# A hybrid decoder layer on one core: product order and gates of the feed-forward, buffers of its down stage, key norms and block inverses of RWKV

## Chip, cores and metric

The kernel runs on 1 core of one Trainium2 chip. The metric is the device time of one execution in microseconds; before the change it is 2186.93 us, the median of 3 runs (2183.86 to 2192.37).

## What is computed

One decoder layer on 1024 tokens of width 1024 in float32: a SwiGLU feed-forward, a mixer, a second feed-forward, each added to the residual, and a final norm. The mixer splits into eight heads of RWKV-7 (a delta-rule recurrence) and a spatial gating unit in chunks of 128 tokens. Cut to what the change touches:

```python
x = x + 0.5 * swiglu(rmsnorm(x, g), w1, w3, w2)     # (silu(h@w1) * (h@w3)) @ w2, twice in the layer
kk = heads(k * k_k)
kk = kk / jnp.maximum(jnp.sqrt(jnp.sum(kk * kk, axis=-1, keepdims=True)), 1e-12)
# per head and token: S_t = S_{t-1} diag(decay_t) + (S_{t-1} a_t) b_t^T + v_t k_t^T ;  y_t = S_t r_t
y = rwkv7_scan(rh, heads(decay), kh, vh, -kk, kk * ah)
```

## The kernel before, in words

Every dense product runs in a split form: an operand is stored as a rounded high part and a low rest (a ScalarE cast and a subtraction on VectorE or GpSimd, the "split"), and three matmuls of 128x128 by 512 columns stand for one.

**Feed-forward.** Tokens come in two halves ("rows") of 512, and the products use a Winograd-Strassen form with seven products. Product 1 and 2 of the way up are made in `first_half` (rows of 512 tokens, eight blocks of weights in turn for w1 and w3, s = 0 to 21), its first part stored to DRAM as `sd`. Meanwhile `build` and `x_build` make the sums of normalised inputs (`xc`) for the other products. Then `up` goes through the 22 weight tiles s (even: w1, odd: w3): `up_prep` takes the weights' sums on VectorE and splits them into five `wup` tiles, TensorE makes products 6, 5, 7, 4, 3 of 12 matmuls each (2.7 us), VectorE adds them to the stored part, and `gate` makes silu of the even tile times the odd one. `out` stores the sums of gated tiles (`hd`). `down` runs seven products of 11 tiles with 12 matmuls each; a tile's weights and inputs land in a `raw` buffer (two of them in the kernel before), are split into `wsp` (four), and after a product VectorE adds the PSUM banks to the residual (line 527). Lines 479 and 480 are the loads, 490 to 493 the splits.

**Mixer.** `w_in_lora`, `w_in_rkv` and `gmlp` make the dense input projection; `pair` (two heads, half the tokens) makes decays, normalised keys and the scaled tensors A, R, B, K. An `Oct` is 128 tokens of all heads: `prep` makes the score matrices and turns, `invert` inverts the 8x8 diagonal blocks on VectorE (by way of DRAM), `merge` joins them to 16, 32 and 64 with small matmuls, `chain` carries the state over chunks of 64, `finish` applies the group norm. `w_out` is the output projection.

**What sets the order.** The program is one generator with side tasks. `Flow` interleaves them by estimated times (the numbers behind `yield`) into one order of matmuls, which TensorE keeps. A planner orders the other engines' instructions; `evac` gives those that read PSUM a higher priority. Each engine works its queue in order. Nearly all loads and stores are issued from SP; RWKV's block moves from ScalarE's queue.

In the second feed-forward `first_half` runs interleaved with the second half of RWKV; at s = 12 at the latest, `second` waits for RWKV, makes the second `w_out` and starts the second `build`.

## Time and profile before

| what | us |
|---|---|
| median of 3 runs | 2186.93 |
| fastest, slowest run | 2183.86, 2192.37 |
| profiled execution | 2188.83 |
| its span, first to last instruction | 2187.0 |
| TensorE busy | 1999.5 (91%) |
| VectorE busy | 1272.0 (58%) |
| GpSimd busy | 987.7 (45%) |
| ScalarE busy | 702.2 (32%) |
| mean granted TensorE clock | 0.956 of full speed |

In the rows, PE is TensorE, PEld its weight loads, DVE VectorE, ACT ScalarE, POOL GpSimd and SP the engine that only issues DMAs; SPq is its queue. L192 is line 192 of the kernel, here the helper that emits every dense matmul, L201 that of the small ones. An operand is written as output<-inputs by the names of the tiles: psd, pse and psc are PSUM banks. A duration of a row with several instructions runs from the first one's start to the last one's end. Matmuls are pipelined, so the busy time of PE is not its peak; some matmul records can be missing.

### The profile page before, as it was taken

The page shows a single profiled execution, that of the slowest core. Times are in us where ns is not written, and L with a number is a line of the kernel's source. Part 1 is how long each engine was busy: PE and PEld are TensorE (multiplying, and loading weights), DVE is VectorE, ACT ScalarE, POOL GpSimd, SP SyncE. Part 2 cuts the span into 40 slices and gives each one's busy share as a digit, 9 for nine tenths or more (in the row PEclk, how much of TensorE's full clock was granted, in tenths as well). Part 3 has the DMA queues.
Part 4 walks back from the last instruction along what each step waited for, and adds up shares of the span by engine and source line. Part 5 has one row for each costly group of instructions (what it writes and reads, how often), then busy time and mean ns, then how long its engine had stood idle before and what let it go on. Part 6 is the DMA issues. An engine that isn't in the chain of part 4 may idle for free.

```text
span 2187.0 us, 34516 instructions
## 1 busy us (share of the span) xinstructions
PE 1999.5 (91%) x13408; PEld 1617.7 (74%) x13408; DVE 1272.0 (58%) x1749; ACT 702.2 (32%) x1202; POOL 987.7 (45%) x749
## 2 busy tenths in 40 slices
PE   6999999997998998999999989989789999979986
PEld 5777777786776677777888778867577777858764
DVE  7828777745457464454543354324877777544565
ACT  5442222213444443252212232224422222224432
POOL 4426666643444664353322232223566666434432
PEclk9999999998998999998999997999989999989988
DMA  6754444435544577453534463336644444375443
GB/s 217 239 170 160 151 160 164 165 141 209 187 135 150 180 258 218 114 202 106 172 101 118 121 191 109 119 112 211 223 148 148 148 158 164 110 251 181 133 153 116
DMA packets 232884, 356.15 MB, mean 163 GB/s; under 512 B 67984, under 2 KB 100752, under 8 KB 232720
## 3 DMA queue, kind: packets, MB, share of 16 engines
q1 hardware_dynamic: 178944, 338.23, 46.5%
q10 hardware_dynamic: 53776, 15.71, 3.1%
q8 instruction: 105, 1.72, 0.3%
q14 instruction: 59, 0.48, 0.1%
HBM read 260.53 MB, written 93.34 MB: 162 GB/s over the span
## 4 chain that ended last, share of the span: by engine, by line
PE 22%; DMA 11%; DVE 8%; issue 5%; POOL 3%; ACT 1%; SPq 0%; POOLq 0%; ACTq 0%; DVEq 0%
PE psd L192 12%; PE pse L192 4%; PE pse L201 3%; DMA raw<-in_ffn_w_dram 3%; DMA raw<-hd 2%; PE psc L201 2%; DMA wraw<-in_ffn_w_dram 1%; POOL wsp L493 1%; DMA raw<-in_w_out_dram 1%; POOL wsp L712 1%; DVE wsp L492 1%; DVE rd L527 1%; POOL wup L257 1%; DMA tdr<-D 1%; DMA M<-ldr 1%
## 5 line engine op out<-in xcount | busy, mean ns | idle before, releaser
L192 PE MATMUL psd<-xt,wsp 128*128 128x512 f32 x1920 | 484.7, 408 | 19.4 <-ACT silu L353 9.0
L192 PEld LDWEIGHTS psd<-xt,wsp 128*128 128x128 f32 x1920 | 363.6, 193 | 115.7 <-ACT silu L353 12.1
L192 PE MATMUL psd<-xc,wup 128*128 128x512 f32 x1584 | 376.0, 394 | 37.2 <-DVE z L447 20.3
L192 PEld LDWEIGHTS psd<-xc,wup 128*128 128x128 f32 x1584 | 298.0, 189 | 108.7 <-DVE z L447 23.8
L712 POOL TENSOR_TENSOR wsp<-raw,wsp 128x512 fp32r<-128x512 f32 x170 | 234.3, 1398 | 317.7 <-ACT wsp L709 317.5
L192 PE MATMUL psd<-wsp 128*128 128x512 f32 x1440 | 351.0, 402 | 27.4 <-ACT wsp L491 14.9
L192 PEld LDWEIGHTS psd<-wsp 128*128 128x128 f32 x1440 | 274.0, 193 | 97.5 <-ACT wsp L491 16.7
L493 POOL TENSOR_TENSOR wsp<-raw,wsp 128x512 fp32r<-128x512 f32 x154 | 210.3, 1368 | 293.7 <-ACT wsp L491 241.3
L257 POOL TENSOR_TENSOR wup<-wraw,wup 128x512 fp32r<-128x512 f32 x132 | 200.6, 1528 | 117.7 <-ACT wup L256 112.4
L192 PE MATMUL pse<-xc,wup 128*128 128x512 f32 x1056 | 248.0, 390 | 0.0
L192 PEld LDWEIGHTS pse<-xc,wup 128*128 128x128 f32 x1056 | 198.4, 188 | 41.4 <-ACT wup L256 0.2
L709 ACT CAST wsp<-raw 128x512 fp32r<-128x512 f32 x246 | 140.5, 618 | 152.5 <-PE psd L192 58.2
L492 DVE TENSOR_TENSOR wsp<-raw,wsp 128x512 fp32r<-128x512 f32 x110 | 96.2, 876 | 104.8 <-ACT wsp L490 104.3
L256 ACT CAST wup<-wraw 128x512 fp32r<-128x512 f32 x132 | 81.1, 619 | 223.5 <-PE pse L192 151.8
L192 PE MATMUL pse<-wsp 128*128 128x512 f32 x396 | 118.3, 416 | 31.2 <-DVE wsp L492 18.1
L491 ACT CAST wsp<-raw 128x512 fp32r<-128x512 f32 x154 | 95.4, 620 | 124.2 <-DMA raw<-hd 114.2
L490 ACT CAST wsp<-raw 128x512 fp32r<-128x512 f32 x110 | 68.0, 618 | 195.2 <-DMA raw<-in_ffn_w_dram 107.8
L192 PEld LDWEIGHTS pse<-wsp 128*128 128x128 f32 x396 | 75.2, 197 | 59.3 <-DVE wsp L492 22.0
L192 PE MATMUL psc<-wsp 128*128 128x512 f32 x396 | 111.6, 408 | 0.0
L257 POOL TENSOR_TENSOR wup<-wt,wup 128x512 fp32r<-128x512 f32 x44 | 63.4, 1440 | 69.7 <-ACT wup L256 58.7
L256 ACT CAST wup<-wt 128x512 fp32r<-128x512 f32 x88 | 53.6, 617 | 120.3 <-PE psd L192 100.9
L192 PEld LDWEIGHTS psc<-wsp 128*128 128x128 f32 x396 | 78.4, 199 | 17.5
(216 smaller groups left out, 2620.6 us busy)
## 6 DMA issues: line engine op xcount, KB each, us to landing
wraw<-in_ffn_w_dram SPq DMA_DIRECT2D x88, 512.0 KB, 4.5
raw<-hd SPq DMA_DIRECT2D x154, 256.0 KB, 3.3
raw<-in_ffn_w_dram SPq DMA_DIRECT2D x132, 256.0 KB, 3.1
raw<-in_ffn_w_dram SPq DMA_DIRECT2D x44, 512.0 KB, 4.0
raw<-in_w_in_dram SPq DMA_DIRECT2D x36, 512.0 KB, 3.6
hd<-u SPq DMA_DIRECT2D x66, 256.0 KB, 2.0
hd<-s SPq DMA_DIRECT2D x66, 256.0 KB, 2.1
sd<-silu SPq DMA_DIRECT2D x44, 256.0 KB, 3.2
```

What stands on the lines that cost most here:

```text
L192: i = self.nc.tensor.matmul(*args, **kw)
L201: i = self.nc.tensor.matmul(*args, **kw)
L256: nc.scalar.copy(t[:, 0], src)
L257: eng.tensor_tensor(t[:, 1], src, t[:, 0].bitcast(F32), op=ALU.subtract)
L490: nc.scalar.copy(t[:, 0, 0], w)
L491: nc.scalar.copy(t[:, 0, 1], h)
L492: ve.tensor_tensor(t[:, 1, 0], w, t[:, 0, 0].bitcast(F32), op=ALU.subtract)
L493: ge.tensor_tensor(t[:, 1, 1], h, t[:, 0, 1].bitcast(F32), op=ALU.subtract)
L527: ve.scalar_tensor_tensor(rv, sets[y][f], 0.25, rv, op0=ALU.mult, op1=ALU.add)
L709: self.nc.scalar.copy(dst[:, 0, sl], src[:, sl])
L712: eng.tensor_tensor(dst[:, 1, sl], src[:, sl], dst[:, 0, sl].bitcast(F32), op=ALU.subtract)
```

## The change

Feed-forward: `gate` applies silu in one ScalarE instruction (the factor at the end becomes 0.5). `up` takes products in the order 6, 5, 7, 3, and 4 after the next tile's 6, each of 6, 5 and 3 in a bank of its own. `down`, `wtile` and `w_out` have four `raw` buffers; scratch tiles of `squares` move to other pools. The normalised inputs of row 0 are stored once (`xn`) by `apply` and loaded by `x_build` instead of normalising again. The second `build` opens its weight pool first and issues the first weight load before `x_build`.

RWKV: squared norms of the keys come from 16 small matmuls by token; their inverse is applied to the score matrix in the mask product and to `Bt` in its PSUM copy, instead of spreading it back and multiplying it into `a`. The block inverse works on 16x16 blocks in 64 partitions: two 8x8 blocks in one instruction, then their off-diagonal part with two products of 512 elements; `merge` has two levels left.

The diff, cut to its core:

```diff
-CON = [("ident", 128), ("me", 128), ("m8", 32), ("m16", 32), ("m32", 32), ...
+CON = [("ident", 128), ("me", 128), ("m16", 32), ("m32", 32), ...
+RAWB = 4
...
     def gate(self, us, pool, s, key, c):
...
-                nc.scalar.activation(u, c, AF.Tanh, scale=0.5)
-                nc.vector.scalar_tensor_tensor(u, u, 1.0, c, op0=ALU.add, op1=ALU.mult)
+                nc.scalar.activation(u, c, AF.Silu)
...
+        ws[3] = sp(b22, ge)
         ws[4] = sp(b21, ge)
-        ws[3] = sp(b22, ge)
...
-        def z(name="z", bufs=6):
+        def z(name="z", bufs=3):
...
-                s1s[s] = z()
+                s1s[s] = z("s1", 3)
...
+        def tail(s, b, w12):
+            yield from prod(s, 4, b, False, True)
             with self.evac():
-                w12 = z()
-                ve.tensor_add(w12, b, s1)
-            yield from prod(s, 5, c, True, False)
-            yield from prod(s, 7, b, False, True)
-            with self.evac():
-                ve.tensor_add(s1, b, s1)
-                w22 = z()
-                ve.tensor_add(w22, c, s1)
-            self.gate(us, u, s, 22, w22)
-            d = self.psum("d")
-            yield from prod(s, 4, d, True, True)
-            with self.evac():
-                ve.tensor_add(s1, d, s1)
-            self.gate(us, u, s, 21, s1)
-            yield from prod(s, 3, c, False, True)
-            with self.evac():
-                ve.tensor_add(w12, c, w12)
-            self.gate(us, u, s, 12, w12)
+                ve.tensor_add(w12, b, w12)
+            self.gate(us, u, s, 21, w12)
             if s % 2:
                 out(s // 2)
             ws.pop(s)
...
+            a = self.psum("d")
+            yield from prod(s, 6, a, True, True)
+            with self.evac():
+                w12 = s1
+                ve.tensor_add(w12, a, s1)
+            if last is not None:
+                yield from tail(*last)
+            c = self.psum("e")
+            yield from prod(s, 5, c, True, True)
+            with self.evac():
+                v = z()
+                ve.tensor_add(v, c, w12)
+            b = self.psum("d")
+            yield from prod(s, 7, b, True, False)
+            with self.evac():
+                w22 = z()
+                ve.tensor_add(w22, b, v)
+            self.gate(us, u, s, 22, w22)
+            d = self.psum("e")
+            yield from prod(s, 3, d, True, True)
+            with self.evac():
+                ve.tensor_add(v, d, v)
+            self.gate(us, u, s, 12, v)
+            last = (s, b, w12)
+        yield from tail(*last)
...
-            raw = self.ws.tile([P, 2, HALF], F32, name="raw", bufs=2)
+            raw = self.ws.tile([P, 2, HALF], F32, name="raw", bufs=RAWB)
...
-                self.squares(self.xq, accs[row], res[row][kp])
+                self.squares(*((self.ws, accs[1], res[1][kp], "raw", RAWB) if row else (pool, accs[0], res[0][kp])))
...
+            if out is not None:
+                nc.sync.dma_start(out[k], t)
...
-            nc.sync.dma_start(t, src[row][k // 2][:, k % 2])
+            nc.sync.dma_start(t, src[row][k // 2][:, k % 2] if row else self.xn[k])
...
-            for k, t in zip(ks, ts):
-                normed(*k, t)
+            for k, t in zip(ks[:2], ts):
+                ve.scalar_tensor_tensor(t, t, self.v(gain, k[1]), rb[0], op0=ALU.mult, op1=ALU.mult)
...
+        if early:
+            self.pw, self.cpw = self.open("pw")
         pool, cb = self.open("pb")
         yield from stats(pool)
+        if early:
+            self.raw0 = self.up_load(self.pw, w, 0)
         yield from self.x_build(pool, self.xc, src, gain, rb)
...
-                    t = self.xq.tile([P, 2, HALF], F32, name="xs", bufs=2)
-                    ts = [t[:, 0], t[:, 1], self.xtp.tile([P, HALF], F32, name="silu", bufs=3)]
+                    ts = [self.xtp.tile([P, HALF], F32, name="silu", bufs=3) for _ in range(3)]
...
-        ss = self.spread2(sq)
-        i8 = self.sm.tile([P, 8], F32, name="i8")
-        ve.tensor_scalar_max(i8, ss, 1e-24)
+        ss = self.psum("e")
+        for i in range(HALF // CH):
+            for s in HS:
+                self.rmm(ss[s, i:i + 1], lhsT=sq[s, i * CH:(i + 1) * CH], rhs=self.one[s], start=(i == 0), stop=True,
+                         skip_group_check=True)
+        i8 = self.inv[half][:, p]
+        ve.tensor_scalar_max(i8, ss[:, 0:HALF // CH], 1e-24)
...
-        inv = self.back2(i8)
...
-        ve.tensor_mul(a, a, inv)
...
+                    for p in range(PR):
+                        k = self.c0 + i
+                        nc.vector.scalar_tensor_tensor(d[:, p], m[:, p], inv[:, p, k:k + 1], c["me"],
+                                                       op0=ALU.mult, op1=ALU.mult)
...
+            K_.nc.vector.tensor_mul(v(t), v(ps), w)
...
-        M = self.tl("M", 1, (P, 8, 8))
+        M = self.tl("M", 1, (64, 16, 16))
...
-        tmp = self.tl("Dtmp", 1, (P, 49))
+        tmp = self.tl("Y2", 1, (P, NB, CH)).rearrange("p b j -> p (b j)")[0:64]
...
+        for l, r, o in ((D[:, 0, 0:8, 0:8], M[:, 0:8, 8:16], Z), (Z, D[:, 0, 8:16, 8:16], D[:, 0, 0:8, 8:16])):
+            nc.vector.tensor_mul(tv, l.unsqueeze(2).broadcast_to([64, 8, 8, 8]),
+                                 r.rearrange("p j k -> p k j").unsqueeze(1).broadcast_to([64, 8, 8, 8]))
+            nc.vector.tensor_reduce(o, tv, axis=AX.X, op=ALU.add)
+            yield 0.6
...
-        for lvl, bs in enumerate((8, 16, 32)):
+        for lvl, bs in enumerate((16, 32)):
```

## Rows read from the trace of the kernel before

**Rows 1.** stages: start:end, length, busy PE, PEld, DVE, ACT, POOL, clock, DMA share, GB/s

```profile
0.00:160.50 160.50, 138.52 (x576) 110.71 (x576) 99.14 (x118) 73.45 (x126) 61.63 (x48) 0.99 0.61 207
160.50:478.30 317.80, 305.98 (x1335) 249.51 (x1336) 238.68 (x276) 83.58 (x142) 193.36 (x132) 1.00 0.44 150
478.30:738.90 260.60, 231.57 (x938) 180.51 (x937) 145.09 (x191) 97.78 (x163) 113.27 (x89) 0.94 0.55 180
738.90:1460.80 721.90, 678.61 (x7838) 558.89 (x7837) 321.52 (x603) 217.99 (x387) 268.28 (x236) 0.94 0.50 151
1460.80:1593.70 132.90, 105.34 (x439) 82.98 (x437) 83.99 (x98) 55.53 (x96) 63.91 (x44) 0.91 0.62 204
1593.70:1909.80 316.10, 307.15 (x1331) 251.44 (x1332) 233.27 (x275) 80.49 (x135) 185.12 (x126) 0.99 0.41 143
1909.80:2166.00 256.20, 226.69 (x935) 178.38 (x933) 141.19 (x179) 91.28 (x152) 101.10 (x75) 0.95 0.53 174
...
sum 2187.00, PE 1999.55 PEld 1617.71 DVE 1271.96 ACT 702.22 POOL 987.67; mean PE 249.94 PEld 202.21 DVE 158.99 ACT 87.78 POOL 123.46
```

**Rows 2.** chain that ended last, 1570 to 1700 us: start, length, what

```profile
1577.04 8.09 DMA wraw<-in_ffn_w_dram
...
1672.87 8.16 PE psd L192 x36
```

**Rows 3.** who TensorE waited for, whole span: us in total, times, longest

```profile
PE psd L192 <- DVE z L447: 20.3, 12, 2.6
...
PE pse L192 <- DVE wsp L492: 18.1, 5, 4.7
...
PE psd L192 <- ACT wsp L491: 14.9, 3, 7.5
...
PE psd L192 <- ACT wup L256: 9.4, 2, 7.6
...
PE pse L201 <- POOL Y L1243: 7.4, 1, 7.4
...
PE psd L192 <- DVE wup L257: 7.2, 2, 7.0
```

**Rows 4.** timeline of the second up stage: start, length, engine, line, [idle before, releaser]

```profile
1740.14 0.69 DVE L386 TENSOR_TENSOR wt<-wraw 128x512 f32<-128x512 f32 x1 [1.40 <-DMA wraw<-in_ffn_w_dram]
...
1744.14 0.68 DVE L447 TENSOR_TENSOR z<-psd,z 128x512 f32<-128x512 f32 x1
...
1744.88 8.00 PE L192 MATMUL psd<-xc,wup 128*128 128x512 f32 x34 [1.48 <-DVE z L447]
```

**Rows 5.** VectorE's instructions by line: busy, mean ns, idle before

```profile
L328 DVE SCALAR_TENSOR_TENSOR u<-u,z 128x512 f32<-128x512 f32 x66 | 61.6, 937 | 23.9 <-ACT u L327 23.9
L328 DVE SCALAR_TENSOR_TENSOR silu<-silu,psd 128x512 f32<-128x512 f32 x22 | 15.0, 682 | 49.9 <-ACT silu L327 39.4 <-DMA sd<-silu 5.6 <-DMA oC<-xC 4.9
L297 DVE SCALAR_TENSOR_TENSOR nx<-nx,vec,rbk 128x512 f32<-128x512 f32 x32 | 33.1, 1050 | 7.2 <-ACT rbk L280 3.6 <-DMA nx<-xres 3.2 <-DMA nx<-in_x_dram 0.4
```

**Rows 6.** line 1043 on ScalarE: ns min/median/max, first and last start

```profile
L1043 ACT ACT_TABLE_LOAD  x2: 1283/1283/1283, 855.9 to 1139.9; - x2
```

**Rows 7.** who SP's queue waited for, 698 to 738 us

```profile
SPq L479 <- DVE wsp L492: 23.2, 9, 5.9
```

**Rows 8.** the page's DMA issues: count, KB each, median us to landing

```profile
raw<-hd SPq DMA_DIRECT2D x154, 256.0 KB, 3.3
```

**Rows 9.** timeline of the second down stage, after its first product

```profile
1949.93 5.46 DVE L527 SCALAR_TENSOR_TENSOR rd<-psd,rd 128x512 f32<-128x512 f32 x9
...
1956.65 1.22 PE L192 MATMUL pse<-wsp 128*128 128x512 f32 x2 [4.28 <-DVE wsp L492]
```

**Rows 10.** timeline of TensorE: small matmuls of RWKV

```profile
781.21 1.05 PE L201 MATMUL pse<-hm,sq 128*128 128x2 f32 x8
...
786.94 1.09 PE L201 MATMUL pse<-con,i 128*64 128x128 f32 x16
...
1287.69 1.12 PE L201 MATMUL pse<-T,SC 64*64 64x32 f32 x32 [0.70 <-DVE D L1146]
```

More of the change, by code (lines that the diff above doesn't have):

```diff
@@ L221, in rstd, with squares @@
         return r[:, :n]
-    def squares(self, pool, acc, t):
+    def squares(self, pool, acc, t, name="xs", bufs=2):
         nc = self.nc
         with self.evac():
-            s = pool.tile([P, 2, HALF], F32, name="xs", bufs=2)
+            s = pool.tile([P, 2, HALF], F32, name=name, bufs=bufs)
             nc.scalar.activation(s, t, AF.Square, scale=1.0 / 32)
@@ L466, in up @@
             ws.pop(s)
+        u = lambda: z("u", 6)
+        prep(0)
+        last = None
+        for s in range(ns):
+            prep(s + 1)
+            s1 = s1s.pop(s)
+            a = self.psum("d")
[23 more added lines that the diff above has]
+        yield from tail(*last)
     def down(self, pool, w2, res, done):
@@ L526, in down, with build @@
                         rv = res[row][k // 2][:, k % 2]
-                        ve.scalar_tensor_tensor(rv, sets[y][f], 0.25, rv, op0=ALU.mult, op1=ALU.add)
+                        ve.scalar_tensor_tensor(rv, sets[y][f], 0.5, rv, op0=ALU.mult, op1=ALU.add)
                     done(p, row, k)
-    def build(self, src, gain, w, rb, stats, ready):
+    def build(self, src, gain, w, rb, stats, ready, early=False):
         self.px, self.cpx = self.open("px")
@@ L571, in program @@
         self.hd = {p: [self.dr.tile([P, HALF], F32, name=f"hd{p}_{j}") for j in range(NP)] for p in range(1, 8)}
+        self.xn = [self.dr.tile([P, HALF], F32, name=f"xn{k}") for k in range(KT)]
         self.sd = [self.dr.tile([P, HALF], F32, name=f"sd{j}") for j in range(2 * NP)]
@@ L580, in program @@
         x12 = self.halves()
-        rbs = [self.keep(rb)]
-        self.apply(x12, rx, "g1", rb)
+        rbs = []
+        self.apply(x12, rx, "g1", rb, self.xn)
         cb.close()
@@ L661, in second @@
             cm.close()
-            yield from self.w_out(1, xres, accs[1])
+            p1, c1 = self.open("p1")
+            yield from self.w_out(1, xres, accs[1], (p1,))
             def stats2(pool):
-                cxq.close()
-                rb = yield from self.spread(accs[1], "e")
-                rbs2.append(self.keep(rb, pool))
-            flow.spawn(self.build(xres[1], "g2", w2, rbs2, stats2, ("xb", 1)))
+                yield 0.1
+                rbs2.append(self.keep(rb1, pool))
+            rb1 = yield from self.spread(accs[1], "e")
+            c1.close()
+            cxq.close()
+            flow.spawn(self.build(xres[1], "g2", w2, rbs2, stats2, ("xb", 1), True))
         yield from self.first_half(x12, w2, hook)
@@ L714, in wtile @@
     def wtile(self, shape, src, eng=None):
-        raw = self.ws.tile([P] + list(shape), F32, name="raw", bufs=2)
+        raw = self.ws.tile([P] + list(shape), F32, name="raw", bufs=RAWB)
         self.nc.sync.dma_start(raw, src)
@@ L733, in dense_T, with w_out @@
         return o
-    def w_out(self, half, xres, acc):
+    def w_out(self, half, xres, acc, sums):
         nc = self.nc
@@ L745, in w_out @@
             for n, k in enumerate([4, 5, 6, 7, 0, 1, 2, 3]):
-                raw = self.ws.tile([P, 2, HALF], F32, name="raw", bufs=2)
+                raw = self.ws.tile([P, 2, HALF], F32, name="raw", bufs=RAWB)
                 nc.sync.dma_start(raw[:, 0], wv[k, :, hc])
@@ L760, in w_out @@
                         nc.vector.tensor_add(r[:, i], r[:, i], ps[2 * j + i])
-                self.squares(self.xq, acc, r)
+                self.squares(*sums[:1], acc, r, *sums[1:])
                 nc.sync.dma_start(xres[1][half][hf * 2 + j], r)
@@ L786, in mixer_consts @@
         self.omk = lambda i: vc[:, 26 + i:27 + i]
-        self.hm = mp.tile([P, 2], F32, name="hm")
-        nc.scalar.copy(self.hm, self.c["bo"][:, 0::64])
-        self.X = [mp.tile([P, NB, CH], F32, name=f"X{i}") for i in range(3)]
+        self.X = [mp.tile([P, NB, CH], F32, name=f"X{i}") for i in range(2)]
         for x in self.X:
@@ L807, in mixer_consts @@
         nc.gpsimd.memset(self.S, 0.0)
+        self.inv = [mp.tile([P, PR, HALF // CH], F32, name=f"inv{h}") for h in range(2)]
         self.pcc = [mp.tile([P, PR, HALF // CH], F32, name=f"pcc{h}") for h in range(2)]
@@ L899, in wrap @@
             yield y
-    def spread2(self, src):
-        ps = self.psum("e")
-        for t in range(4):
-            self.rmm(ps[:, 2 * t:2 * t + 2], lhsT=src[:, t * P:(t + 1) * P], rhs=self.hm,
-                     start=(t == 0), stop=True, skip_group_check=True)
-        return ps[:, 0:8]
-    def back2(self, small):
-        ps = self.psum("e")
-        for t in range(4):
-            for h in range(2):
-                self.rmm(ps[HS[h], t * P:(t + 1) * P],
-                         lhsT=small[:, 2 * t + h:2 * t + h + 1].broadcast_to([P, CH]), rhs=self.c["ident"],
-                         start=True, stop=True)
-        return ps
     def pair(self, half, p, k, v, r):
@@ L1091, in prep @@
         yield 2.5
+        inv = K_.inv[self.half]
         SC = self.SC = self.tl("SC", 2, (P, 2, NC, PR, 2, CH))
@@ L1113, in prep, with turned @@
         yield 0.5
-    def turned(self, name, X):
+    def turned(self, name, X, scale=None):
         K_ = self.K
@@ L1177, in merge @@
             pt = K_.psum("e", (P, 2, NB, CH // 2))
-            for n in range(1 if lvl == 2 else 2):
+            for n in range(1 if lvl == 1 else 2):
                 for b in range(NB):
@@ L1184, in merge @@
                             K_.rmm(pt[s, 1, b], lhsT=T[s, 0, b], rhs=one(X[s, b], 0), start=True, stop=True)
-            for n in range(1 if lvl == 2 else 2):
+            for n in range(1 if lvl == 1 else 2):
                 d = part(T[:, n], 1 - n)
```

64 lines of the change are left out of this document (34 added, 30 removed).

## The prediction, made before the change was timed

> **What bounds the kernel now.** I read the stages first [rows 1]. TensorE is busy 1999.6 of 2187.0 us, so the only large gains are its idle time, its slow clock and work taken off it. One full-speed matmul of 512 columns costs 8.16 us / 36 = 0.2267 us [rows 2]; its count times that is the floor of a stage:
> - first "up" stage (160.5 to 478.3): 1335 records, floor 302.6, measured 317.8, 15 over;
> - second "up" stage (1593.7 to 1909.8): 1331 records, floor 301.7, measured 316.1, 14 over;
> - "down" stages: 7 products x 11 tiles x 12 = 924 matmuls, floor 209.5; measured 260.6 and 256.2, so 51 and 47 over. The granted clock there is 0.94 and 0.95: (1 - 0.94) x 260.6 = 16 us and 13 us of that can be the slow clock;
> - the mixer (738.9 to 1460.8): 7838 matmuls, mostly small ones of RWKV, between the dense ones;
> - the passage to the second "up" (1460.8 to 1593.7): about 413 big matmuls, 94 us, and 2 us of small ones in 132.9: 37 over.
>
> Then who TensorE waits for [rows 3]. 20.3 us go to the VectorE add of line 447, 18.1 and 14.9 us to the splits of the down stage, 7.5 us of it in one stretch; 9.4 and 7.2 us to the first operands of an up stage. The clock falls after such stretches, so a wait removed returns more than its own length.
>
> **Up: product order.** Product 7 accumulates in the bank that product 6 has filled and line 447 has to read first; between them lies only product 5 (12 x 0.2267 = 2.7 us). VectorE works in order, and in front of line 447 stand the weight sums of the next tile, which wait for their load [rows 4]: line 386 starts at 1740.14 when the load lands, line 447 only at 1744.14, TensorE goes on at 1744.88 after 1.48 us of waiting. In the new order 6 has a bank of its own that nobody needs soon; the only bank accumulated into after a read is that of 7, and product 3 and the next tile's product 6 (5.4 us) lie between the read (w22) and product 4. What delayed line 447 here was about 4 us, so most of these waits disappear. The add count stays at five a tile. The smaller pools (z and s1 3, s 4) hold two z and four s tiles per one or two tiles of 13.6 us; I cost them at nothing, since their last readers are done a tile earlier; if not, a wait is that of a store, some 3 us. I leave 5 us over the floor in each stage: **-10** and **-9** (ends -15 and +5: nothing gained, and a late tile every now and then).
>
> **Gates.** Silu in one ScalarE instruction replaces tanh plus a VectorE instruction: 66 x 0.94 + 22 x 0.68 = 77 us of VectorE work leave [rows 5], all beside TensorE; this only shortens the queue in front of the adds. It is in the numbers of the stages. New table loads: one costs 1283 ns [rows 6]; with two more (silu, and back to tanh for the mixer) +2.6, I write **+2** (0 to +4). The Trainium skill (ScalarE: Activation LUTs, "Table sets") puts exp and tanh into one set, does not name silu there, and says to batch calls by set, which speaks against this edit. By its 2.66 us a switch the same two would be an estimated 5.3 us; no run here shows the drain it counts with the load.
>
> **Down: four raw buffers for two.** A raw buffer is reloaded only after its last split. In product 4 of the first down stage the load's issue waits 23.2 us of 40 for VectorE's split to free a buffer [rows 7]; a load lands 3.3 us after its issue [rows 8], and a pair of buffers must turn round in 2 x 2.72 us. So the stage runs at the rate of the buffers, not of an engine: VectorE, ScalarE and GpSimd are busy 145, 98 and 113 of 260.6 us [rows 1]. With four, loads run two tiles further ahead. At the start, loads of the residual and of the eleven dt tiles stand in front, and TensorE waits up to 7.5 us [rows 3]; two tiles more in hand cover 5.4 us of it. Between products nine to twelve evacuations occupy VectorE (nine took 5.46 us, then TensorE had waited 4.28 us for a split [rows 9]); more splits can stand ready (four, 10.9 us). What I leave: 2 us at the start, 4 at the evacuations, 5 for the statistics matmuls, 5 ragged, 7 of clock: 23 of 51. **-28**, and **-26** for the second. In product 4 of the first stage one raw buffer holds the sums of squares of row 1, leaving three. Ends: -10 (the start cover alone) and -36 for each.
>
> **Mixer.** Merge level 8 goes: 96 matmuls an octet, 8 octets. 32 of them take 1.12 us [rows 10], so 96 x 8 / 32 x 1.12 = 27 us of TensorE. The Trainium skill (TensorE: Matmul & The Clock Gate, Part 1) states a floor of about 25 ns from start to start; by it the same 768 would be an estimated 19 us, while the row here gives 35 ns each. The key norms lose 8 matmuls (1.05 us) and 16 (1.09 us) a pair and get 32 small ones (nearest row 1.12 us): -2.14 + 1.12, times 8 pairs, -8 us. Together 35 us off TensorE's stream, which is busy 678.6 of 721.9 us here. VectorE gets the 8 x 8 products of the inverse (two of 512 elements and their sums, about 0.7 us each by the 512-element row of 0.68 us [rows 5]), the Bt scaling and masks in quarters, loses 3 merge evacuations and one product by the norm; it is busy 45%, so only latency counts: about +3 us of VectorE and -4.5 us of a merge level for each octet, equal within 2 us. Bt leaves ScalarE's queue, where it stood behind DMA issues: a small gain. Against: lora_up's three silu tiles serve one iteration instead of two, 8 iterations behind a store of some 3.3 us [rows 8], 26 us of ScalarE waiting at most, mostly under prepared splits: +4; and the scratch of the inverse shares the buffer Y2 with the group norm: 0 to 5 us for each of 8 octets, I take +1 in all. Sum **-30** (ends -50 and +5, this also being a stage whose hand-written order shifts).
>
> **Passage to the second up.** The build of its inputs runs on VectorE; 16 of 32 normalising products (33.1 us / 32 = 1.03 us each [rows 5]) leave, eight of them here: -8 us. The weights' load is issued only after the build and takes 8.09 us [rows 2]; TensorE waits for the operands 7.6 and 7.0 us [rows 3]. It now starts before the build: -12. Four raw buffers in the output projection: -2. **-22** (-30 to -6).
>
> **Start** (0 to 160.5): eight normalising products and eleven gate instructions less on VectorE (16 us) beside TensorE; **-4** (-10 to +4). The 16 stores of 256 KB of normalised inputs run on SP's queue at DMA shares of 0.61 and 0.62 [rows 1]: nothing; if they get in front of weight loads, one landing, 3 us. End (from 2166.0): 0.
>
> **Sum.** -4 -10 -28 -30 -22 -9 -26 +2 = -127. The profiled execution took 2188.8 us (span 2187.0), so 2062; it lies 1.9 above the median of 2186.93: **2060**.
>
> **Rivals.**
> 1. *The downs stay as they are.* Splits and evacuations in one VectorE queue, not the buffers, set the pace; only the start's cover of 5 us each remains. 54 - 10 = 44 back: **2104**. For it: the waits for VectorE's split of 4.28 us after evacuations. Against: that engine is busy little over half of the stage, and the issue waits for a buffer.
> 2. *The mixer gives nothing.* TensorE's stream is shorter, but waits for the same chain (oct load, inverse, merge, chain, norm) and for Y2; in the row with 7.4 us it waits for GpSimd's norm product at the very end [rows 3]. **2090**.
> 3. *Slower.* In the new order the read of w22 falls behind the weight sums on VectorE, in every tile. Whatever it is late beyond the 5.4 us of cover, TensorE stands, 44 times; 127 / 44 = 2.9 us, so from a read 8.3 us late in every tile the whole gain is gone; at 10 us it is 44 x 4.6 = 202 us in place of the 19 hoped for: about **2280**. Against: the delay seen is 4 us, with fewer VectorE instructions to come.
> 4. *It is not what the stages wait for:* every wait is replaced and the time stays at **2187**.
>
> **How the numbers follow.** Forecast 0.66 (own range 2022 to 2095), rival 1 0.15, rival 2 0.13, rival 3 0.04, rival 4 0.02. The range takes in the forecast, rival 2 and most of rival 1: 2020 to 2112. About 0.5% (11 us) is what a measurement of this kernel can tell from no change; so faster 0.94, same 0.02, slower 0.04.
>
> **What would show it.** Right: no waits on the first add of a tile, up stages at 307 us; down stages near 232 with a clock of 0.97 or more; 768 matmuls fewer of the 64x32 form; the weights' load of the second up before its build. Wrong: SP's loads no longer waiting for buffers but down stages still at 250 (rival 1), the mixer at 720 with longer waits (rival 2), waits for w22's add of several us in each tile (rival 3).

## The result, and the profile after

The kernel after takes 2123.4 us (median; 2119.3 to 2130.3), the kernel before, timed beside it, 2185.4 (2178.1 to 2192.4): ratio 0.972, 95% interval 0.968 to 0.976. It is 62 us faster, where 127 were forecast (2060), and lies above the range of 2020 to 2112. The profiled execution took 2130.3 us, span 2128.5; it is the longest of the four runs, 7 us above their median. Every row of a stage below is of one execution, up to 7.5 us from the median of its kernel. The kernel before had medians from 2180.8 to 2185.4 us beside the different runs, so two totals that lie less than 5 us apart are not told apart.

The stages of the kernel after, with columns as in [rows 1] (start:end, length, busy time of TensorE, its loads, VectorE, ScalarE and GpSimd, granted clock, DMA share, GB/s):

```profile
0.00:158.50 158.50, 136.51 (x576) 112.31 (x576) 85.57 (x99) 73.64 (x126) 59.02 (x48) 0.99 0.68 229
158.50:461.10 302.60, 302.35 (x1332) 249.94 (x1333) 187.29 (x243) 84.25 (x142) 175.84 (x129) 1.00 0.48 159
461.10:702.90 241.80, 220.54 (x939) 178.74 (x940) 158.42 (x190) 93.91 (x161) 127.54 (x91) 0.95 0.57 192
702.90:1451.30 748.40, 659.99 (x7137) 545.69 (x7137) 354.24 (x652) 216.41 (x382) 276.36 (x236) 0.90 0.51 149
1451.30:1574.50 123.20, 106.88 (x434) 86.55 (x432) 74.27 (x85) 51.53 (x90) 54.34 (x38) 0.90 0.61 205
1574.50:1878.70 304.20, 303.29 (x1332) 249.69 (x1333) 185.32 (x243) 82.93 (x142) 178.43 (x129) 1.00 0.48 158
1878.70:2108.60 229.90, 219.82 (x937) 178.96 (x936) 146.48 (x179) 89.49 (x153) 114.89 (x78) 0.96 0.56 188
```

Line by line against [rows 1], measured and forecast:

```
stage        before   after   change   forecast
start         160.5   158.5     -2.0      -4
first up      317.8   302.6    -15.2     -10
first down    260.6   241.8    -18.8     -28
mixer         721.9   748.4    +26.5     -30
passage       132.9   123.2     -9.7     -22
second up     316.1   304.2    -11.9      -9
second down   256.2   229.9    -26.3     -26
```

Outside the mixer the stages give -84 where -99 was forecast (+2 more were allowed for table loads). The mixer alone is 56 us off. In its row TensorE has 701 instructions and 18.6 us of busy time less than before, and yet the stage is longer: idle time rose from 43 to 88 us, and the granted clock fell from 0.94 to 0.90. The stretches at 1.2 GHz add up to 150 us there, before to 85. The question of the experiments is therefore where the 35 us of TensorE work went.

Whom TensorE waits for in the mixer of the kernel after (waiting instruction, releaser: us in all, times, longest):

```profile
PE pse L202 <- DMA AR<-xR: 9.3, 3, 3.2
PE pse L202 <- POOL Y L1273: 7.6, 2, 7.4
PE pse L202 <- DVE D L1169: 7.4, 2, 6.3
PE pse L202 <- issue: 6.7, 2, 6.2
PE pse L202 <- DVE SC L1107: 6.4, 4, 2.8
```

No one wait took over. The norm product Y cost the kernel before as much (7.4 us [rows 3]), and so did the loads of AR:

```profile
PE pse L201 <- DMA AR<-xR: 9.3, 3, 5.1
```

New or longer are many small ones on VectorE's steps: the inverse (D), the masks (SC), and more of about 5 us and less.

### The profile page after: what moved, and what is told of

It reads as the page before. It is cut to its first block, busy times and chain, and to the rows that moved or that the text cites. A ratio compares the mean times of both kernels' runs of the same rounds, so it can differ in the third digit from the quotient of the medians.

```text
span 2128.5 us, 33099 instructions
## 1 busy us (share of the span) xinstructions
PE 1954.6 (92%) x12704; PEld 1606.7 (75%) x12704; DVE 1200.3 (56%) x1701; ACT 693.7 (33%) x1194; POOL 987.4 (46%) x748
## 5 line engine op out<-in xcount | busy, mean ns | idle before, releaser
L193 PEld LDWEIGHTS psd<-xt,wsp 128*128 128x128 f32 x1920 | 374.9, 198 | 103.7 <-DVE wsp L731 5.5
L731 POOL TENSOR_TENSOR wsp<-raw,wsp 128x512 fp32r<-128x512 f32 x170 | 237.2, 1415 | 326.3 <-ACT wsp L728 326.2
L193 PE MATMUL psd<-wsp 128*128 128x512 f32 x1440 | 344.9, 400 | 15.2 <-ACT wsp L501 9.3
L503 POOL TENSOR_TENSOR wsp<-raw,wsp 128x512 fp32r<-128x512 f32 x154 | 230.2, 1500 | 214.7 <-ACT wsp L501 165.7
L193 PE MATMUL pse<-xc,wup 128*128 128x512 f32 x1056 | 254.4, 389 | 0.0
L258 POOL TENSOR_TENSOR wup<-wraw,wup 128x512 fp32r<-128x512 f32 x132 | 180.5, 1378 | 118.2 <-ACT wup L257 117.3
L502 DVE TENSOR_TENSOR wsp<-raw,wsp 128x512 fp32r<-128x512 f32 x110 | 107.3, 986 | 79.9 <-ACT wsp L500 79.5
L385 DVE TENSOR_TENSOR wt<-wraw 128x512 f32<-128x512 f32 x44 | 42.1, 957 | 187.7 <-DMA wraw<-in_ffn_w_dram 187.7
L500 ACT CAST wsp<-raw 128x512 fp32r<-128x512 f32 x110 | 68.2, 620 | 185.8 <-PE psd L193 57.8
L193 PE MATMUL pse<-wsp 128*128 128x512 f32 x396 | 113.0, 414 | 14.0 <-DVE wsp L502 8.7
L193 PE MATMUL psc<-wsp 128*128 128x512 f32 x396 | 105.8, 396 | 1.8 <-DVE wsp L502 1.8
L731 DVE TENSOR_TENSOR wsp<-raw,wsp 128x512 fp32r<-128x512 f32 x76 | 63.9, 872 | 75.3 <-ACT wsp L728 71.4
L193 PEld LDWEIGHTS pse<-wsp 128*128 128x128 f32 x396 | 78.5, 201 | 34.8 <-DVE wsp L502 12.3
```

What stands on the lines that cost most here:

```text
L193: i = self.nc.tensor.matmul(*args, **kw)
L258: eng.tensor_tensor(t[:, 1], src, t[:, 0].bitcast(F32), op=ALU.subtract)
L385: ve.tensor_sub(t1, b12, b11)
L500: nc.scalar.copy(t[:, 0, 0], w)
L502: ve.tensor_tensor(t[:, 1, 0], w, t[:, 0, 0].bitcast(F32), op=ALU.subtract)
L503: ge.tensor_tensor(t[:, 1, 1], h, t[:, 0, 1].bitcast(F32), op=ALU.subtract)
```

## Experiments 1: the parts one by one

V is the inverse from blocks of 16, N the key norms by token, F all of the feed-forward part (gates, order of products, buffers, row statistics).

**V undone** (e1_no_v): `invert`, `merge` and the constants as before.

```diff
-        for lvl, bs in enumerate((16, 32)):
+        for lvl, bs in enumerate((8, 16, 32)):
...
-        M = self.tl("M", 1, (64, 16, 16))
+        M = self.tl("M", 1, (P, 8, 8))
...
```

> The kernel after, but with inverses from blocks of 8 and three merge levels as before (key norms by token and all of the feed-forward part stay). Theory P (pace: the mixer is as long as its chain of RWKV steps; work taken off TensorE comes back as waits): 2123 +- 8 us, mixer 740 to 755 us, TensorE busy there about 25 us more than the 660 of the kernel after and idle as much less. Theory V (the longer inverse on 64 partitions, 9.2 us in place of 4.4 for each octet, is what the mixer lost): 2095 to 2105, mixer about 720. Theory N (key norms by token cost it): 2123 + 0 to 25. Theory F (the feed-forward part's side effects on the mixer cost some 55 us, and the RWKV part gives the forecast 30): about 2145, mixer 770.

**N undone** (e2_no_n): `pair`, the mask products and `turned` as before.

```diff
-        ss = self.psum("e")
-        for i in range(HALF // CH):
...
+        ss = self.spread2(sq)
...
+        inv = self.back2(i8)
...
```

> The kernel after, but with the key norms as before (eight spreading and sixteen back-spreading products a pair, one mask product for each B half, Bt copied by ScalarE); the inverse from blocks of 16 and the feed-forward part stay. Theory P: 2123 +- 8 us, mixer 740 to 755. Theory N (masks in quarters and Bt on VectorE lengthen the way to the inverse): 2095 to 2110, mixer 720 to 735. Theory V: 2123 to 2135. Theory F: 2130, since some 8 us of TensorE come back.

**Both undone** (e3_no_nv): the two edits together, which leaves F alone.

> The feed-forward part alone: the kernel after with both RWKV parts undone. Theory P: 2115 to 2130 us, mixer 735 to 755, with fewer waits and more work on TensorE. Theories V and N: 2090 to 2100, mixer 715 to 725 as in the kernel before. Theory F: 2145 to 2160, mixer 770 to 785.

**Only V and N** (e4_rwkv_only), **only V** (e5_v_only), **only N** (e6_n_only): the same edits made to the kernel before, nothing of F.

> The kernel before with both RWKV parts and nothing of the feed-forward part. Theory P: 2178 to 2195 us (before 2185), mixer 715 to 730 with TensorE busy 35 us less and idle 35 us more than before. Theories V and N: 2205 to 2215, mixer 745. Theory F: 2150 to 2160, mixer 690 to 695.

> The kernel before with the inverse from blocks of 16 alone. In the feed-forward version this part was worth 2 to 4 us (2111.3 against 2113.5, and 2123.4 against 2127.1), with some 19 us of TensorE work less in the mixer and 16 us more of its waits. Theory P (the mixer's pace is set by the RWKV steps, so that such work comes back as waits): 2173 to 2185 us, mixer 714 to 724, TensorE busy there about 655 and idle 60 to 65. Rival (TensorE's work counts where the order written by hand is the old one): 2155 to 2165, mixer 695 to 705.

> The kernel before with the key norms by token alone. In the feed-forward version this part cost 13.6 us (2127.1 against 2113.5) and, beside the other inverse, 12.1 (2123.4 against 2111.3). Theory N1 (it costs by itself: four mask instructions for one, and Bt on VectorE, on the way of each of 8 octets): 2190 to 2198 us, mixer 733 to 740. Theory N2 (it costs only where the feed-forward part has moved the order of the instructions): 2165 to 2182, mixer 708 to 722.

Measured (us; total is the median, that of the kernel before over 19 runs, the rest is the mixer of the profiled run, from the end of the first down stage to the first product of the second output projection):

```
parts     total    mixer  TensorE busy   idle   at 1.2 GHz
none     2184.5    722.4     679.1       43.3      85.5
V        2182.4    716.1     649.9       66.2      79.5
N        2180.2    719.8     661.0       58.8      79.2
V N      2173.4    714.1     635.5       78.6      92.7
F        2113.5    734.6     678.2       56.4      84.9
F V      2111.3    731.0     659.0       72.0      98.3
F N      2127.1    748.3     672.1       76.2     116.9
F V N    2123.4    748.4     660.0       88.4     150.2
```

What follows:
- F alone makes all of the gain, 2113.5 us, and costs the mixer 12 us all the same.
- Work that V and N take from TensorE comes back as waits. Without F both together take 43.6 us of busy time (forecast 35) and give back 35.3 us of idle time, so the stage shortens by 8. Theory P had the direction (2173.4 us lies below its 2178 to 2195), and rival 2 of the prediction its reason.
- V is worth 2 to 7 us in all four places (alone, with a ratio to before of 0.9975 to 1.0017, it is not told from nothing), N between a gain of 9 and a loss of 14: 2182.4 to 2173.4 beside V, but 2111.3 to 2123.4 beside F and V. Theories V and N (one part costs some 25 us by itself) both fall: e2 alone came near what N gave for it (2111.3 us, mixer 731), but e4 and e6 are faster than before, not slower. F's side effects account for 12 us, not 55.
- With F, N's loss is not in idle time, which rises by 16 to 20 us as it does without F (12 to 16). It is in TensorE's busy time, which should fall by 14 to 18 us and falls by 6 or not at all while 32 to 52 us more pass at 1.2 GHz.

## Experiments 2: the down and up stages

**Two raw buffers** (e7_raw2):

```diff
-RAWB = 4
+RAWB = 2
```

> The kernel after with two raw buffers in place of four. Theory B (the turn-round of the buffers set the pace of the down stages): the second down stage goes back from 230 to 250-258 us, the first from 242 to 255-265 (row 1's squares use a raw buffer there, so it can be worse than before); total 2160 to 2180. Rival S (the splits and evacuations on VectorE set it, and it was the lighter VectorE that helped): second down stage 228 to 236, total 2120 to 2132. The mixer, too, uses these buffers: if early loads get in front of RWKV's loads there, it becomes shorter than 748 by some 5 to 12 us.

2214.6 us (2209.1 to 2216.1), ratio to before 1.014 (1.011 to 1.016). Its two down stages, columns as above:

```profile
461.50:755.80 294.30, 241.25 (x938) 183.37 (x936) 151.89 (x190) 96.54 (x160) 116.49 (x91) 0.91 0.47 157
1932.30:2193.20 260.90, 230.26 (x938) 179.63 (x936) 146.18 (x179) 91.40 (x153) 105.58 (x78) 0.94 0.51 170
```

31 us more in the second and 52 in the first, with VectorE as busy as with four buffers. Theory B holds, with more lost than it said (255 to 265 us for the first stage, 2160 to 2180 in all), rival S and with it rival 1 of the prediction fall: the turn-round of the buffers set the pace. In the first stage row 1's squares take raw buffers in the new code, which fits its higher price; that this is all of it was not tried. The mixer (743.6 us) gains 5 at most, so early weight loads are not what it suffers from.

**Gates as before** (e8_tanh):

```diff
-                nc.scalar.activation(u, c, AF.Silu)
+                nc.scalar.activation(u, c, AF.Tanh, scale=0.5)
+                nc.vector.scalar_tensor_tensor(u, u, 1.0, c, op0=ALU.add, op1=ALU.mult)
...
-                        ve.scalar_tensor_tensor(rv, sets[y][f], 0.5, rv, op0=ALU.mult, op1=ALU.add)
+                        ve.scalar_tensor_tensor(rv, sets[y][f], 0.25, rv, op0=ALU.mult, op1=ALU.add)
```

> The kernel after with the gates as before (tanh on ScalarE and one more VectorE instruction for each of 44 gates), the new order of the products and additions kept. Theory O (the order did it): up stages stay at 302 to 305 us, total 2119 to 2130. Rival G (the lighter VectorE did it: 33 us less in each up stage): up stages go back to 310-316 us each, total 2138 to 2150.

2141.8 us (2136.9 to 2147.2), 18 more than after. Its up stages, and TensorE's largest wait in the first:

```profile
161.10:472.70 311.60, 306.35 (x1332) 250.20 (x1333) 233.50 (x276) 82.59 (x142) 180.84 (x129) 0.99 0.45 154
1580.50:1894.90 314.40, 306.85 (x1332) 250.19 (x1333) 233.60 (x276) 82.12 (x142) 182.17 (x129) 0.99 0.45 152
```

```profile
PE psd L193 <- DVE z L469: 5.0, 8, 0.7
```

The new order leaves 311.6 of 317.8 us, the silu takes the stage to 302.6. Rival G holds for most of the gain: with 234 us of work VectorE still reaches the adds late (eight waits of up to 0.7 us), with 187 it doesn't. The new gates in the old order were not run, so the two shares hold in this sequence only. The trace of the kernel after has seven table loads of 1283 ns against four in this one, and is the faster by 18 us. The Trainium skill (ScalarE: Activation LUTs, "Table sets") says to batch calls by set, which speaks for the tanh; here three loads cost less than 88 VectorE instructions (66 in the up stages, 22 in `first_half`).

## Experiments 3: the order of the mixer

The steps of RWKV have a place among the dense products that a clock in the program gives when the instructions are written out: each step's planned pause is added and rounded up to a tick of 2.4 us. Each part of the change alters what that clock counts, so the steps that stay fall elsewhere too.

**The clock shifted** in the kernel after (e10_shift) and before (e11_shift_before): no instruction added or removed.

```diff
+        flow.now += 1.2
         self.mp, cm = self.open("mp")
```

> The kernel after, with the clock of the order written by hand moved on by 1.2 us (half a tick) at the start of the mixer; no instruction is added or removed, the RWKV steps only fall between other dense products. Theory L (luck of the order: how steps fall among the dense products is worth as much as the parts themselves): the mixer moves by 8 to 25 us either way, total outside 2116 to 2131. Rival (the costs are of the steps themselves): mixer 748 +- 6, total 2117 to 2130.

> The kernel before with the same shift of 1.2 us. Theory L: mixer off by 8 us or more from 722, total under 2176 or over 2193. Rival: mixer 722 +- 6, total 2177 to 2192.

After: 2114.7 us (2114.0 to 2117.4), 8.7 less than after, and none of its runs is as slow as the fastest of after. Its mixer:

```profile
702.50:1438.40 735.90, 646.23 (x7136) 532.27 (x7136) 352.64 (x652) 215.84 (x382) 273.67 (x236) 0.92 0.51 152
```

Idle time is as in the kernel after (90 us); busy time is 13.8 us less, with 113 us at 1.2 GHz instead of 150. So one microsecond at the lower level cost 13.8 / 36.8 = 0.38 us here, and the 65 us more that after has over before come to some 20 to 25 us of its 56. (The ratios to before, 0.969 here and 0.972 for after, have intervals that overlap.) In the kernel before the shift changes nothing: 2188.6 us (2174.0 to 2193.3), mixer 719.7, interval of the ratio 0.998 to 1.004. Theory L holds for one of the two kernels, and not for a third order: with N undone the shift moves the total by 3.7 us (2111.3 in e2, 2107.6 in e14 below).

**Dense products first** (e9_dense_first): row 1's statistics get a wait on the first dense tile and stay behind its last product.

```diff
             yield 1.0
+            if row:
+                yield ("dense", 0)
+                self.hold = self.last
...
         p0 = yield from self.dense_T(self.w_cols(w, 12), xt)
+        self.flow.done.add(("dense", half))
```

> The kernel after, with row 1's statistics products (one,raw) put behind the first 24 dense products of the mixer instead of in front of all of them (a wait in the order written by hand; it moves the later order a little too). In the kernel after TensorE does no dense work for 8.5 us from 702.9, in the kernel before it goes on at once. Theory: the position costs what TensorE waits there (4.0 us for the squares) and the products behind it: 3 to 6 us less, gap 3 to 5 us, total 2116 to 2121. Rival: the first dense weights aren't there sooner (their load is issued 4.7 us before the stage begins, in the kernel before 6.3): gap 7 to 9 us, 2121 to 2127. A change of over 10 us either way would mean that the moved order of the rest counts more than the gap.

TensorE at the start of the mixer, first in the kernel after, then in this one (start, length, instruction, count, idle time ahead of it and releaser):

```profile
702.81 1.09 PE L817 MATMUL pse<-wT,ones 128*64 128x128 f32 x16
707.95 3.57 PE L202 MATMUL pse<-one,raw 128*128 128x1 f32 x16 [4.05 <-DVE raw L233]
711.38 2.91 PE L193 MATMUL psd<-xt,wsp 128*128 128x512 f32 x6
```

```profile
703.99 1.09 PE L826 MATMUL pse<-wT,ones 128*64 128x128 f32 x16
706.71 0.73 PE L193 MATMUL psd<-xt,wsp 128*128 128x512 f32 x2 [1.62 <-ACT wsp L737]
708.07 6.19 PE L193 MATMUL psd<-xt,wsp 128*128 128x512 f32 x19 [0.62 <-POOL wsp L740]
```

The start gap goes from 8.5 to 2.6 us, so the weights were there. The total is 2109.6 us (2106.2 to 2112.7), 13.8 less than after and more than the theory's 3 to 6: by its own sign the moved order of the rest counts for more than the gap. The mixer has 729.1 us, 642.1 of them busy. Its idle time, 87.0 us, is only 1.4 less than in the kernel after, so what the gap gave came back as other waits; busy time is 17.9 us less, with 106 us at 1.2 GHz in place of 150.

**A longer planned pause** (e12_plan_longer), in the kernel after, behind each inverse:

```diff
-        yield 6.0
+        yield 10.8
```

> The kernel after, with 4.8 us (two ticks) more planned between each octet's inverse and its first merge product, so that more dense products stand between them. Theory A (the planned pause is too short for the inverse on 64 partitions, so TensorE stands in order before a step that isn't ready): waits on the inverse and merges fall, mixer 725 to 740, total 2100 to 2115. Theory C (the chain of octets itself is the bound: each octet later by what is added): 8 x 4.8 = 38 us at most, mixer 755 to 785, total 2130 to 2160. Between them, 2117 to 2130: the dense products only change places with waits.

2118.7 us (2114.9 to 2123.0), mixer 743.1, idle 94.9: between the two theories, neither shown; the dense products changed places with waits.

**N undone in the two other orders** (e13_first_no_n on e9, e14_shift_no_n on e10):

> The kernel with the dense products first (2109.6 us), key norms as in the kernel before. Undoing the key norms gained 12.1 us in the order of the kernel after, and in the kernel before they were worth 3 to 4 us the other way. Theory N1 (by token they cost 10 to 15 us by themselves in the feed-forward version): 2094 to 2100 us, mixer 712 to 718. Theory N2 (it was the place of the steps in that one order): 2104 to 2116, mixer 725 to 735.

> The kernel after with the clock of the order moved by 1.2 us (2114.7), key norms as before. Theory N1: 2099 to 2105 us. Theory N2: 2107 to 2120. Together with 2111.3 for the same kernel without the shift it also says how far 1.2 us moves a second order: theory L, by 8 us and more; otherwise within 5.

2115.0 us (2111.7 to 2121.5) and 2107.6 (2102.6 to 2110.0): N gains 5 us in the first order, costs 7 in the second and 12 in that of the kernel after. N2 holds; N has no price of its own that these runs can tell from the luck of the order.

**Without the inverse's arithmetic** (e15_first_no_inv, on e9):

```diff
-        for t in range(1, 8):
...
-            nc.vector.tensor_reduce(o, tv, axis=AX.X, op=ALU.add)
-            yield 0.6
+        nc.vector.tensor_add(D[:, 0], D[:, 0], M)
+        for t in range(6):
+            yield 0.6
```

> The kernel with the dense products first, the 18 VectorE instructions of each octet's inverse left out but for one addition (the planned pauses stay; the output is that of a first approximation of the inverse). 8 x some 7 us of VectorE work go, all on the way from the masks to the merge. Theory A (the mixer waits for the longer inverse): 2090 to 2100 us, mixer 708 to 718. Theory P (the steps keep the places that the order gives them, so a step that is ready sooner gains only the waits that named it): 2102 to 2110, mixer 722 to 730.

2073.5 us (2071.9 to 2075.0), 36 less than e9 for 47 us less of VectorE work (352 to 305 in the mixer). Its mixer:

```profile
701.00:1398.90 697.90, 631.32 (x7137) 522.30 (x7137) 305.28 (x516) 216.39 (x382) 274.80 (x236) 0.94 0.53 160
```

Idle time is 20 us less than in e9 and busy time 11 less, at the same number of products. Theory A has the direction, and its size (10 to 20 us) is passed: VectorE's inverse is not beside the path. (The order of the later steps changed with it, so not all of the 36 us need be the inverse's own. And nearly half of this arithmetic is not the change's: the inverse takes VectorE 56 us in the kernel after and 26 in the kernel before.) How it stands in the way is seen on VectorE in the kernel after around 1208 us:

```profile
1208.37 0.15 DVE L1168 TENSOR_TENSOR Y<-D,M 64x2 f32<-64x2 f32 x1 [3.73 <-DMA M<-ldr]
1209.66 0.68 DVE L1107 TENSOR_TENSOR SC<-pse,con 128x512 f32<-128x512 f32 x1
1210.62 0.41 DVE L1203 TENSOR_TENSOR X<-pse,con 128x256 f32<-128x256 f32 x1
```

```profile
1210.48 1.97 PE L202 MATMUL pse<-con,Y 64*64 64x64 f32 x32 [6.28 <-DVE D L1169]
```

The inverse's first instruction holds VectorE for 3.73 us until its load lands (28.8 us over the octets, 20.8 in the kernel before; 29.9 with V undone, e1, and 24.4 with F alone, e3, so it is not the longer inverse that makes this wait), and the masks that empty TensorE's small banks (SC, X) stand behind it in the queue, between its 18 instructions. TensorE waits 6.28 us. That these waits in VectorE's queue are what all of TensorE's new idle time comes from is argued from places like this one, not shown.

**A tick of 1.2 us** (e16_first_tick, on e9), **the same with V undone** (e17_tick_no_v), **and in the kernel before** (e18_tick_before):

```diff
-TICK = 2.4
+TICK = 1.2
```

> The kernel with the dense products first, with the tick of the order's clock at 1.2 us in place of 2.4: every planned pause of an RWKV step was rounded up to 2.4, now to 1.2. Theory P (the planned pauses pace the octets, whose chain ends the mixer): mixer 700 to 720, total 2080 to 2100. Rival (the pauses are what the other engines need; a step placed earlier makes TensorE wait in order): mixer 729 to 745, idle above 95 us, total 2108 to 2125.

> The kernel with the dense products first and the tick of 1.2 us (2079), with the inverse from blocks of 8 and three merge levels as before. At a tick of 2.4 undoing it made no difference (2127.1 against 2123.4), TensorE's extra work and the shorter wait being equal. Theory A (leaving the arithmetic of the inverse out gained 36 us, so some 5 us of it for each octet are worth 15 to 20, as much as the merge level's TensorE time): 2070 to 2085. Rival (with finer pauses the mixer is bounded by TensorE's work, 25 us more of it counts): 2095 to 2110, mixer 715 to 730.

> The kernel before with the tick of 1.2 us. Theory P (the rounded pauses paced the octets of the kernel before too, so nothing that only shortens a step could shorten its mixer): 2150 to 2168 us, mixer 695 to 710 in place of 722. Rival (in the kernel before, with 43 us of waits, TensorE's work was the bound; the pauses bind only after work has left): 2175 to 2192, mixer 715 to 725.

2079.0 us (2073.1 to 2082.7; ratio to before 0.953, 0.950 to 0.956), 2109.7 (2106.2 to 2116.4) and 2210.4 (2202.7 to 2217.6; ratio 1.012). The first is faster than both kernels of this change. Mixer and passage together, up to the first product of the second up stage, in this order (the output projection and the dense products of the passage mix here, so that the mixer has no end of its own in the last two):

```profile
697.30:1519.20 821.90, 743.39 (x7570) 605.65 (x7569) 421.27 (x737) 266.55 (x472) 326.36 (x274) 0.94 0.54 167
```

```profile
702.10:1561.00 858.90, 776.28 (x8334) 631.32 (x8334) 405.18 (x729) 266.49 (x472) 323.48 (x274) 0.94 0.51 159
```

```profile
741.20:1608.80 867.60, 787.76 (x8274) 638.54 (x8273) 408.75 (x698) 270.85 (x479) 318.89 (x275) 0.94 0.50 155
```

In the kernel after the same stretch (702.9 to 1574.5) has 871.6 us, in the kernel before (738.4 to 1584.5) 846.1. With the finer tick all three have a clock of 0.94. The first mixer alone (697.3 to 1397.1) has 699.8 us, 638.7 busy and 61.1 idle: 22.6 less than before, near the -30 of the forecast. V, worth 4 us in the order of the kernel after, is worth 31 here: without it TensorE is busy 33 us longer and idle about as long (82.6 us of the stretch against 78.5). In this order the work taken off TensorE did leave the stage, as the prediction had it (27 us for V). Theory A is wrong there, its rival right. And theory P is wrong of the kernel before: finer pauses make it 26 us slower, past its rival's 2175 to 2192 too, with 16.4 us of waits for the masks (2.6 in the mixer of the kernel before) and 15.2 for sums of squares:

```profile
PE pse L201 <- DVE SC L1102: 16.4, 4, 5.2
PE pse L201 <- DVE xs L232: 15.2, 3, 9.2
```

So the pauses' rounding is not a toll that every order pays. What it is in the fine order that suits the longer inverse and not the shorter one stays open.

## Why the prediction was half right

**Mixer: -30 forecast, +26.5 measured; the step that failed.** The counting was good: at the price of the clock above, TensorE's work at full speed went from 679 - 0.35 x 85 = 649 to 660 - 0.35 x 150 = 607 us, so 42 us left where 35 were counted (0.35 lies between the 0.38 of e10 and the 21.3 / 71.7 = 0.30 of e16, both against after). What failed is the step from "35 us off TensorE's stream" to "Sum -30": it took a stage with 43 us of idle time, in-order waits and a clock of 0.94 for a list of products and subtracted from the list. 45 us came back as idle time and some 23 as slower clock: -42 + 45 + 23 = +26, in one execution that lies 7 us above its median. Four parts of that can be told:
- V and N give back 35 us of waiting without F (e4) and 32 beside it (e3 against after).
- "Only latency counts: about +3 us ... equal within 2 us" was wrong about VectorE. The four block instructions take 3.6 us an octet, as estimated or nearly:

```profile
L1175 DVE TENSOR_TENSOR Y<-D,M 64x512 f32<-64x512 f32 x8 | 9.3, 1161 | 0.2
L1175 DVE TENSOR_TENSOR Y<-Z,D 64x512 f32<-64x512 f32 x8 | 8.7, 1087 | 0.2
L1177 DVE TENSOR_REDUCE Z<-Y 64x64 f32<-64x512 f32 x8 | 5.4, 676 | 0.2
L1177 DVE TENSOR_REDUCE D<-Y 64x64 f32<-64x512 f32 x8 | 5.4, 675 | 0.2
```

  But VectorE is not judged by its 45% of busy time. Others' evacuations stand behind these, and e15 prices the arithmetic of the inverse at up to 36 us of the total for 47 us of work. The change added 30 us of it, and 33 us to VectorE's work in the mixer, 4.1 an octet for the 3 forecast: the size was nearly right, that it costs no more than its own latency was not.
- The start gap of 8.5 us was not in the sum: row 1's statistics stand in front of the first dense products and wait there for their squares, in the kernel before behind 27 of them (e9).
- The order: 9 to 14 us of the total lie in where the steps fell (e10, e9), nearly all of it as busy time at the lower clock. That is luck of this order: the same shift moved the kernel before by nothing and the kernel without N by 3.7 us.

The terms for lora_up's tiles and the scratch shared with Y2 (+4 and +1) were not measured by themselves.

**Down: -28 and -26; -18.8 and -26.3.** The reason was right and is shown by e7. The first stage misses 9 us, most of it at one place: before product 4, 35 us from the stage's end, TensorE stands for 7.44 us.

```profile
658.97 2.47 DVE L537 SCALAR_TENSOR_TENSOR res<-pse,res 128x512 f32<-128x512 f32 x4
661.36 2.47 DVE L537 SCALAR_TENSOR_TENSOR res<-psc,res 128x512 f32<-128x512 f32 x4
664.41 1.23 DVE L233 TENSOR_TENSOR raw<-raw 128x1024 f32<-128x1024 f32 x1 [0.58 <-ACT raw L231]
665.55 0.69 DVE L497 TENSOR_TENSOR raw<-raw,dt 128x512 f32<-128x512 f32 x1
665.66 0.33 SPq L489 DMA_DIRECT2D raw<-in_ffn_w_dram  x1
666.33 0.62 ACT L500 CAST wsp<-raw 128x512 fp32r<-128x512 f32 x1 [1.95 <-DVE raw L497]
```

```profile
667.52 27.92 PE L193 MATMUL psd<-wsp 128*128 128x512 f32 x110 [7.44 <-ACT wsp L501]
```

The sum for the next tile (L497), which the split of L500 needs, stands in VectorE's queue behind eight evacuations (4.9 us) and row 1's squares (0.58 us of waiting for ScalarE and 1.23 us of work). The prediction had 4 us for the evacuations of a stage; the squares in this queue it had at nothing. It had also seen that row 1's squares leave three raw buffers, and put no price on it: a load does wait 7.5 us for that buffer, but goes out at 665.66, after L497 has begun, so it is not what TensorE waits for here.

**Up: -10 and -9; -15.2 and -11.9.** The floor of 302.6 is reached and that of 301.7 missed by 2.5 us; of the 5 us a stage that I left, none and half were needed. The reason was half wrong: the order alone brings the first stage 6.2 us and leaves the second within 2 of [rows 1], and the gates, which had no number of their own in the sum, bring 9 and 10 us (e8). They were the work in front of the adds. Rival 3, the late read of w22, did not come.

**Passage: -22; -9.7.** The early load did its part: waits of 7.6 and 7.0 us for the first operands [rows 3] fell to 1.8 and 0.2, -12.6 for -12. But row 1's statistics, which ran in the build before, now stand between the output projection and the dense products:

```profile
1506.37 3.57 PE L202 MATMUL pse<-one,xs 128*128 128x1 f32 x16 [4.26 <-DVE xs L233]
1511.29 2.08 PE L202 MATMUL pse<-con,rr_r 128*128 128x128 f32 x8 [1.35 <-POOL rr_r L221]
1513.01 7.18 PE L193 MATMUL psd<-xt,wsp 128*128 128x512 f32 x24
```

From the last product of the projection to the next dense one are 10.9 us, before 4.8. The eight normalising products that left the build gave nothing that can be seen: the build is hidden by 216 dense products.

**Start and end:** -2.0 and -1.1, as small as said. Rival 2's mechanism was the true one for V and N, at a price of 56 us against the forecast instead of 30, 12 of them from F.

## What to carry to other kernels

In a stage that already has idle time and a clock below full, work taken from the busiest engine is not time taken from the stage: count what the engines that answer it must do in their own order, and give the stage a bound that includes its present waits. Where an order is written out by a planned clock, run a version with the clock shifted before you put a price on a part; here half a tick was worth 9 us in one order and 4 or nothing in two others, and one part was worth 4 us in one order and 31 in another. A statistics step in front of dense work is looked for at each boundary that a change moves: at two of them here TensorE went some 6 us longer without dense work. Moving one away gave 14 us, but not as 6 us of waits less: time the move, don't subtract the gap.

## What the runs showed of the hardware

- The same 7136 to 7138 products of the mixer took these busy times of TensorE in seven executions:

```
run          after     e7     e8    e12    e10     e9    e16
busy us      660.0  655.0  655.1  648.2  646.2  642.1  638.7
at 1.2 GHz   150.2  143.1  133.5  128.4  113.4  106.3   78.5
```

  A straight line through them rises by 0.30 us for each microsecond at the lower level (0.38 without e16), and all seven lie within 3 us of it. Six dense products in a row lost more: 2.93 us at 1.2 GHz (kernel before, from 1593.65) against 1.52 us at 2.4 GHz (kernel after, from 502.96), 0.48 us for each microsecond. That it is the waits between the small products that lose nothing is argued, not shown.
- VectorE's 64 x 512 products with repeated and strided operands took 1161 and 1087 ns in the mean, where mask products of 128 x 512 took 680. Means mislead here: plain 128 x 512 products of two tiles vary from 680 to 1786 ns (u<-u,z). The shortest and the median of the eight (ns, minimum, median, maximum) say more:

```profile
L1175 DVE TENSOR_TENSOR Y<-D,M x8: 999/1026/2128, 855.6 to 1353.7; 64x512 f32<-64x512 f32 x8
L1175 DVE TENSOR_TENSOR Y<-Z,D x8: 1003/1006/1589, 857.4 to 1356.0; 64x512 f32<-64x512 f32 x8
L329 DVE TENSOR_TENSOR u<-u,z x44: 680/1074/1786, 183.8 to 1874.3; 128x512 f32<-128x512 f32 x44
```

  The Trainium skill (VectorE: DVE Perf Modes, "Mode 1× (REGULAR) — the baseline") says that this mode works with any strides, at one result a cycle; here none of the sixteen products went below 1.47 times the shortest plain one. The rows don't tell the strides' part from that of the repeated operands.
